# Log-gate sums carried as rows of the score operands, one-step normalisation helpers, and recurrent states kept at pairs of chunks

## The chip, the cores and the metric

The kernel runs on one core of a Trainium2 chip. The metric is the device time of one execution in microseconds (us). TensorE is PE in the profile (its weight loads PEld), VectorE is DVE, ScalarE is ACT, GpSimd is POOL, and SyncE, which issues the DMAs, is SP.

## The reference, cut to what matters

A sequence of 512 tokens of width 1024 goes through two blocks. The first has a short-convolution layer and a forgetting-attention layer (16 heads of 64), each followed by a gated feed-forward layer and a layer norm. The second normalises by root mean square, mixes with four latent-attention heads and four gated-linear-attention heads that run forward and backward, and ends in a feed-forward layer and an output gate. All of it is in float32. The parts that the change touches:

```
# forgetting attention, a head h: F is the running sum of log f over the tokens
logits[t, s] = q[t] . k[s] * 0.125 + F[t] - F[s]      (s <= t, else -inf)
p = softmax(logits)

# gated linear attention, chunks of 64 tokens, in each of two directions
b = cumsum(log f) inside a chunk
o_intra = (mask * (q*exp(b-b_mid)) @ (k*exp(b_mid-b)).T) @ v
state   = exp(b_last) * state + (k*exp(b_last-b)).T @ v       # one step for each chunk
o_inter = (q*exp(b)) @ state_before

rms_norm(x)   = x * rsqrt(mean(x*x) + eps) * g
layer_norm(x) = (x - mean) * rsqrt(var + eps) * g + b
```

## The kernel before

**Layout.** Activations lie transposed, features on the 128 partitions and the 512 tokens along the row. A product in full precision is three matmuls of operands split into a high and a low part (`mm3`); weights stream from DRAM in units of eight 128x128 blocks (`_make_unit`): one DMA into `raw`, a cast to `whi` on ACT, and a subtraction to `wlo` on DVE or POOL.

**Order.** Nothing is issued as it is written. A recorder takes down every operation, `cost` (line 291) gives it a price by engine and size, and `plan` (line 365) is a list scheduler that walks through a modelled time: each engine takes the ready operation that stands first in the program, buffers and PSUM banks are counted in ledgers, and a tensor-tensor operation of DVE can be given to POOL when DVE's queue is long (`to_pool`). The result is one fixed order for each engine, SP's DMAs included. All instructions therefore carry one line in the profile, 575, and are told apart by the names of their tiles. Changing an operation or a price redraws the order everywhere.

**Forgetting attention** (`fox_block`, line 1238). The projections that give the log gates (`pf`), two key tiles (`pk0`, `pk1`) and the first values (`pv`) run together over the tiles `hk` that the layer norm before delivers; `rest` then makes the query inputs `hq`. The gate goes through log-sigmoid to a running sum `F` of 16 heads (line 1267), which is stored to DRAM as `fd` and also transposed by PE into `fneg` (lines 1274 to 1278). The score step `fox_scores` (line 1390) handles a pair of heads: for each head the row of `F` is read back from `fd` to all 128 partitions (`Fb`), `Fm` adds the causal mask of a diagonal block, and for each of four query blocks `i` two matmuls write S (with the opposite sign), DVE builds the deviation `G` in one or two `tensor_scalar` operations and then adds it to S and takes the minimum in one `tensor_tensor_reduce`; ACT exponentiates:

```
if i:
    nc.vector.tensor_scalar(G[:, :i * P], Fb[hh][:, :i * P], self.fneg[:, i, h:h + 1], None, ALU.add)
nc.vector.tensor_scalar(G[:, tb], Fm[hh][:, tb], self.fneg[:, i, h:h + 1], None, ALU.add)
nc.vector.tensor_tensor_reduce(G[:, :N], s[:, :N], G[:, :N], 1.0, BIG, ALU.add, ALU.min, negm[hh][:, i:i + 1])
```

The second of the two score matmuls multiplies the low part of k (`k..l`, one tile for both heads) with a query tile (`q..az`, `q..bz`) whose other 64 rows are zero (`fox_k`, `fox_q`). `fox_values` transposes the probabilities (`tp`, `PT`) and multiplies with the values (`po`). The eight pairs are recorded so that the scores of pair f+1, the keys and queries of pair f+2 and the values of pair f interleave.

**Normalisation** (`newton_rsqrt`, line 793; `rms_rstd`, line 809). Four layer norms (each in two halves of 256 tokens) and 17 root-mean-square norms (512 tokens) take a logarithm, an exponential and a square on ACT and then three operations on DVE (tiles `..a`, `..r`); a root-mean-square norm first moves its PSUM sum to `..v` on DVE. `split_scaled` (line 881) makes the high part of a normalised tile on ACT, its full value `..e` on DVE, and the low part on DVE.

**Gated linear attention** (`gla_prep`, `gla_scores`, `gla_states`, lines 1818 to 1905). For each of 4 heads and 2 directions there are 8 chunks: 7 matmuls with 64 rows give the chunk products `..kv`, the states `..st` follow one another on DVE (one copy on ACT, then 6 multiply-adds), and each state enters the output `gpo` by a matmul with 64 columns. `B2_ORDER` (line 30) is the recorded order of the steps of these heads and of the four latent-attention heads (`proj`, `score`, `value`).

Of the kernel before, what the change touches and what calls it, by code (L numbers as in the profile page):

```python
# [6 lines left out]
F32 = mybir.dt.float32  # L7
# [152 lines left out]
class Part:  # L160


    def __init__(self, tile, key, rows):
        self.tile, self.key, self.rows, self.cast = tile, key, rows, None
# [5 lines left out]
    def region(self):  # L170
        return (*self.rows, 0, 1)
# [7 lines left out]
class DramRef(TileRef):  # L179
    def __getitem__(self, key):  # L180
        k = key[0] if isinstance(key, tuple) else key
        rows = (k, k + 1) if isinstance(k, int) else (k.start, k.stop)
        return Part(self, key, rows)

    def all(self):
        return Part(self, None, (0, self.shape[0]))
# [7 lines left out]
class Recorder:  # L194
# [96 lines left out]
    def cost(self, op, ins, outs):  # L291
# [11 lines left out]
        if op.eng == "PE":  # L303
# [3 lines left out]
            if dt == F32:  # L307
                return 4 + max(4 * size / 2.4, 156)
# [280 lines left out]
class Build:  # L589
# [203 lines left out]
    def newton_rsqrt(self, v, name, r=None):  # L793
# [3 lines left out]
        r0 = self.f(name + "r0", sh)  # L797
        self.act(r0, v, AF.Ln)
        self.act(r0, r0, AF.Exp, scale=-0.5)
        a = self.f(name + "a", sh)  # L800
        nc.scalar.activation(a, r0, AF.Square)
# [79 lines left out]
    def split_scaled(self, d, g, b, hl, sl, name):  # L881
# [4 lines left out]
        nc.vector.tensor_scalar(e, d[:, sl], g, b, ALU.mult, ALU.add)  # L886
# [37 lines left out]
    def setup(self):  # L924
# [37 lines left out]

        self.cmask = self.c("cmask", (P, 1, P))
        nc.gpsimd.memset(self.cmask, 0.0)
        nc.gpsimd.affine_select(self.cmask, self.cmask, [[0, 1], [-1, P]], ALU.is_ge, 1.0e30,
                                base=0, channel_multiplier=1)
        self.one_col = self.c("one_col", (P, 1))
        nc.gpsimd.memset(self.one_col, 1.0)
        self.tiny_col = self.c("tiny_col", (P, 1))
        nc.gpsimd.memset(self.tiny_col, 1.2e-19)  # L970
# [263 lines left out]
    def fox_block(self, kva, qa, rest, ln):  # L1234
# [33 lines left out]
        fd = self.dram("fd", (H, T))  # L1268
        nc.sync.dma_start(fd.all(), F)
# [4 lines left out]
        tp = self.ps("s", "Ftp", (P, 4, H))  # L1274
# [7 lines left out]
        probs = self.fox_scores(0, q[0], ks[0], fd)  # L1282
        q.append(self.fox_q(1, qa))
        for f in range(8):
# [8 lines left out]
            if f < 7:  # L1293
                probs = self.fox_scores(f + 1, q[f + 1], ks[f + 1], fd)
# [18 lines left out]
    def fox_k(self, f, kva, pk=None):  # L1313
# [3 lines left out]
        ka, kb, kl = (self.r(f"k{f}{n}") for n in ("a", "b", "l"))  # L1317
        top, bot = slice(0, 64), slice(64, P)
        if pk is None:
            pk = self.out(f"pk{f}")  # L1320
            self.gemm_all([("w_k", f, pk)], kva)
        for ps, sl in pk:
            nc.scalar.copy(kb[:, sl], ps)
            nc.scalar.copy(ka[top, sl], ps[top])
            nc.scalar.copy(ka[bot, sl], ps[top])
            nc.vector.tensor_tensor(kl[:, sl], ps, kb.bitcast(F32)[:, sl], ALU.subtract)
            nc.scalar.copy(kb[top, sl], ps[bot])
        return ka, kb, kl
# [43 lines left out]
    def fox_q(self, f, qa):  # L1372
# [6 lines left out]
        q = [self.r(f"q{f}{n}") for n in ("a", "b", "az", "bz")]  # L1379
        halves = slice(0, 64), slice(64, P)  # L1380
        for hh in range(2):
            own, other = halves[hh], halves[1 - hh]

            nc.gpsimd.memset(q[2 + hh].bitcast(F32)[other], 0.0)
# [667 lines left out]
```

## Time and profile before

| | before |
|---|---|
| median of 3 runs | 1939.76 us (1939.32 to 1940.83) |
| profiled execution, its own time | 1939.52 us |
| span of its profile | 1937.8 us |
| PE, PEld busy | 1893.9 us (98%), 1593.3 us (82%) |
| DVE, ACT, POOL busy | 1284.3 (66%), 817.4 (42%), 190.3 us (10%) |
| mean granted TensorE clock | 0.989 of full speed |
| forgetting attention | about 572 to 843 us of the span |
| mixer of the second block | about 1215 to 1486 us of the span |

The span runs from the first to the last instruction; the time of the execution is 1.7 us longer. A busy PE says that a matmul was in flight, not that it ran at full clock: the windows below carry the granted clock of each stretch beside the busy time. A matmul of float32 operands shows as two records.

### The profile page before, as it was taken

The page shows a single profiled execution, that of the slowest core. Times are in us where ns is not written, and L with a number is a line of the kernel's source. Part 1 is how long each engine was busy: PE and PEld are TensorE (multiplying, and loading weights), DVE is VectorE, ACT ScalarE, POOL GpSimd, SP SyncE. Part 2 cuts the span into 40 slices and gives each one's busy share as a digit, 9 for nine tenths or more (in the row PEclk, how much of TensorE's full clock was granted, in tenths as well). Part 3 has the DMA queues.
Part 4 walks back from the last instruction along what each step waited for, and adds up shares of the span by engine and source line. Part 5 has one row for each costly group of instructions (what it writes and reads, how often), then busy time and mean ns, then how long its engine had stood idle before and what let it go on. Part 6 is the DMA issues. An engine that isn't in the chain of part 4 may idle for free.

```text
span 1937.8 us, 24555 instructions
## 1 busy us (share of the span) xinstructions
PE 1893.9 (98%) x9382; PEld 1593.3 (82%) x9382; DVE 1284.3 (66%) x2208; ACT 817.4 (42%) x1344; POOL 190.3 (10%) x148
## 2 busy tenths in 40 slices
PE   9999999999999989999999999999999999999999
PEld 7888888888888778898888888877877888888887
DVE  8877976566579788894533335999898644334445
ACT  5322523122346667553322232686684533123333
POOL 0000100000010332210000000132151000000000
PEclk9999999999999899999999999999998999999999
DMA  9675277566434112323222222422111222222232
GB/s 350 224 249 173 99 241 251 187 233 228 142 108 153 58 64 88 120 66 131 99 94 96 97 98 79 140 82 82 44 55 44 98 98 98 98 98 94 94 139 76
DMA packets 76470, 245.55 MB, mean 127 GB/s; under 512 B 8496, under 2 KB 9776, under 8 KB 76352
## 3 DMA queue, kind: packets, MB, share of 16 engines
q1 hardware_dynamic: 76352, 243.98, 36.6%
q8 instruction: 73, 1.20, 0.3%
q14 instruction: 45, 0.37, 0.1%
HBM read 235.53 MB, written 8.42 MB: 126 GB/s over the span
## 4 chain that ended last, share of the span: by engine, by line
PE 57%; DVE 7%; ACT 2%; issue 1%; DVEq 0%; ACTq 0%
PE pu L575 12%; PE pg L575 12%; PE pd L575 9%; PE gt L575 4%; PE ffn_down L575 2%; PE wo L575 2%; PE pl L575 2%; PE attn_o L575 1%; DVE axr L575 1%; PE pv L575 1%; PE po L575 1%; PE pq L575 1%; PE MS L575 1%; PE tp L575 1%; PE pk L575 1%; PE S L575 1%
## 5 line engine op out<-in xcount | busy, mean ns | idle before, releaser
L575 ACT CAST whi<-raw 128x1024 fp32r<-128x1024 f32 (+1 forms) x313 | 326.1, 1043 | 598.5 <-PE pd L575 139.1
L575 DVE TENSOR_TENSOR wlo<-raw,whi 128x1024 fp32r<-128x1024 f32 (+1 forms) x286 | 349.8, 1224 | 321.0 <-ACT whi L575 316.9
L575 POOL TENSOR_TENSOR wlo<-raw,whi 128x1024 fp32r<-128x1024 f32 x27 | 65.4, 2423 | 1281.7 <-ACT whi L575 1251.5
L575 DVE CUSTOM_DVE_ANT_0 aj<-ada,cact,adab 128x1024 bf16<-128x1024 f32 x96 | 126.3, 1322 | 30.0 <-DMA ada<-in_wada 29.4
L575 DVE TENSOR_TENSOR s<-pu,s 128x512 f32<-128x512 f32 x44 | 30.1, 689 | 76.5 <-PE pu L575 76.5
L575 DVE TENSOR_TENSOR S<-S,sq 128x512 f32<-128x512 f32 (+1 forms) x62 | 36.7, 591 | 1.6 <-ACT sq L575 1.4
L575 ACT ACTIVATE s<-s 128x512 f32<-128x512 f32 x22 | 13.9, 632 | 54.1 <-DVE s L575 54.1
L575 ACT ACTIVATE s<-pg 128x512 f32<-128x512 f32 x44 | 26.0, 591 | 23.2 <-PE pg L575 23.0
L575 DVE CUSTOM_DVE_ANT_0 G<-S,G 128x128 f32<-128x128 f32 (+3 forms) x64 | 30.6, 484 | 1.6 <-PE S L575 0.9
L575 DVE TENSOR_TENSOR xr<-pd,xr 128x512 f32<-128x512 f32 x16 | 11.0, 690 | 26.9 <-PE pd L575 26.9
L575 DVE TENSOR_SCALAR G<-Fm,fneg 128x128 f32<-128x128 f32 x64 | 25.9, 410 | 0.9 <-PE po L575 0.5
L575 ACT ACTIVATE sq<-axr 128x256 f32<-128x256 f32 (+1 forms) x33 | 15.1, 466 | 23.1 <-DVE axr L575 23.1
L575 DVE TENSOR_SCALAR G<-Fb,fneg 128x128 f32<-128x128 f32 (+2 forms) x48 | 23.6, 491 | 1.3 <-ACT Pa L575 0.6
L575 DVE TENSOR_TENSOR s<-pg,rfr 128x512 f32<-128x512 f32 x22 | 15.2, 691 | 12.0 <-PE pg L575 12.0
L575 DVE TENSOR_TENSOR u<-pu,rfr 128x512 f32<-128x512 f32 x22 | 15.2, 691 | 11.8 <-PE pu L575 11.7
L575 POOL TENSOR_TENSOR Fm<-Fb,cmask 128x512 f32<-128x512 f32 x14 | 18.6, 1334 | 27.7 <-DVE PT_2l L575 9.1
L575 PE MATMUL tp<-ident,Pa 128*128 128x128 f32 x64 | 17.2, 294 | 3.2 <-DVE Pa L575 3.1
L575 PE MATMUL pg<-hm0l,whi 128*128 128x512 f32 (+1 forms) x48 | 18.0, 376 | 1.9 <-DVE hm0l L575 1.9
L575 PE MATMUL pg<-hm0h,whi 128*128 128x512 f32 (+1 forms) x48 | 18.0, 378 | 1.3 <-ACT hm0h L575 1.3
L575 ACT ACTIVATE Pa<-G,negm 128x128 f32<-128x128 f32 (+1 forms) x32 | 16.2, 505 | 6.8 <-DVE negm L575 4.7
L575 ACT ACTIVATE sq<-x 128x256 f32<-128x256 f32 (+1 forms) x19 | 9.8, 518 | 21.6 <-DVE x L575 21.5
L575 PE MATMUL pg<-hm0h,wlo 128*128 128x512 f32 (+1 forms) x48 | 18.0, 376 | 0.6 <-DVE wlo L575 0.6
(3680 smaller groups left out, 6298.7 us busy)
## 6 DMA issues: line engine op xcount, KB each, us to landing
raw<-in_wpack SPq DMA_DIRECT2D x309, 512.0 KB, 3.5
ada<-in_wada SPq DMA_DIRECT2D x96, 512.0 KB, 4.2
ada<-in_wada SPq DMA_DIRECT2D x32, 256.0 KB, 6.0
Fb<-fd SPq DMA_DIRECT2D x16, 256.0 KB, 4.5
x<-in_xT SPq DMA_DIRECT2D x8, 256.0 KB, 6.0
pd<-pple SPq DMA_DIRECT2D x8, 256.0 KB, 6.0
xd<-x SPq DMA_DIRECT2D x8, 256.0 KB, 2.6
axr<-xd SPq DMA_DIRECT2D x8, 256.0 KB, 5.1
```

The costliest lines, as they stand in the source:

```text
L575: getattr(getattr(nc, op.unit), op.name)(*[get(x) for x in op.args], **{k: get(x) for k, x in op.kw.items()})
```

## The change

- **Scores.** `F` is split into a high and a low part and both rows of a head are stored in `fd`. A new helper `beside` makes, for each head, the q and k tiles of the second score matmul: 64 rows hold the low part of k (or the query), and of the other 64 rows, 32 are all -1 (k) or +1 (q) and 32 are zero but for the two rows of `F`, which a DMA brings from `fd`. The matmul itself then adds F[s] - F[t]. `Fb`, `Fm`, `fneg`, the transposes of `F` and all the `tensor_scalar` operations on `G` go; the `tensor_tensor_reduce` reads a fixed mask of 512 columns, shifted by block. There are now two low-part tiles of k in place of one.
- **Norms.** `newton_rsqrt` takes two operations on DVE in place of three, ACT scales once more, and the root-mean-square norms read their sum from PSUM with no `..v`. The full value `..e` in `split_scaled` moves from DVE to ACT.
- **States.** Keys and queries are decayed to the edges of pairs of chunks, so that there are 3 matmuls with 128 rows for the products, 2 multiply-adds after one copy, and 3 matmuls with 128 columns into `gpo` for each head and direction. The part from one chunk of a pair to the other is computed in `gla_scores` by 4 more matmuls of 64x64, and two POOL memsets in `mla_scores` open these regions in the mask. `gla_prep` has six products of 256 elements where it had two of 512, and one small product for the pair's decay.
- **Prices** in `cost`: float32 matmuls of few columns 193 for 156, `tensor_tensor_reduce` 112 for 180, a price for the scan.

```diff
@@ cost
-                return 4 + max(4 * size / 2.4, 156)
+                return 4 + max(4 * size / 2.4, 193)
...
-            return 180 + 1.0417 * size + 61 * cols
+            return 112 + 1.0417 * size + 61 * cols
...
+        if n == "tensor_tensor_scan":
+            return 68 + 2.0833 * size
@@ newton_rsqrt(self, v, name, r=None, n=1.0, eps=0.0)
         nc.scalar.activation(a, y, AF.Square)
-        nc.vector.tensor_tensor(a, a, v, ALU.mult)
-        nc.vector.tensor_scalar(a, a, -0.5, 1.5, ALU.mult, ALU.add)
+        nc.scalar.mul(y, y, -0.5 / n)
+        if eps:
+            nc.vector.scalar_tensor_tensor(a, v, n * eps, a, ALU.add, ALU.mult)
+        else:
+            nc.vector.tensor_tensor(a, a, v, ALU.mult)
...
-        nc.vector.tensor_tensor(r, a, r0, ALU.mult)
+        nc.vector.scalar_tensor_tensor(r, a, 3.0 * n, y, ALU.subtract, ALU.mult)
@@ rms_rstd
-        v = self.f(name + "v")
-        nc.vector.tensor_scalar(v, s, 1.0 / n, EPS, ALU.mult, ALU.add)
-        return self.newton_rsqrt(v, name)
+        return self.newton_rsqrt(s, name, n=float(n), eps=EPS)
@@ split_scaled
-        nc.vector.tensor_scalar(e, d[:, sl], g, b, ALU.mult, ALU.add)
+        nc.scalar.activation(e, d[:, sl], AF.Identity, bias=b, scale=g)
@@ fox_block
-        fd = self.dram("fd", (H, T))
-        nc.sync.dma_start(fd.all(), F)
+        fd = self.dram("fd", (H, 2, T))
+        for i, x in enumerate(self.split(F, "Fx")):
+            nc.sync.dma_start(fd[0:H, i], x.bitcast(F32))
...
-        for i in range(4):
-            nc.tensor.transpose(tp[:, i, :], F[:, i * P:(i + 1) * P], self.ident[:H, :H])
-        self.fneg = self.c("fneg", (P, 4, H))
-        nc.scalar.mul(self.fneg, tp, -1.0)
@@ fox_k
+        low = [self.beside(2 * f + hh, "k", -1.0) for hh in range(2)]
         for ps, sl in pk:
...
+            for hi, lo, own, other in ((ka, low[0], top, bot), (kb, low[1], bot, top)):
+                nc.scalar.copy(hi[own, sl], ps[own])
+                nc.vector.tensor_tensor(lo[own, sl], ps[own], hi.bitcast(F32)[own, sl], ALU.subtract)
+                nc.scalar.copy(hi[other, sl], ps[own])
+    def beside(self, h, name, first):
+        nc = self.nc
+        t = self.r(f"{name}z{h}")
+        o = 64 * (1 - h % 2)
+        ones, sums = (o, o + 32) if name == "k" else (o + 32, o)
+        nc.gpsimd.memset(t.bitcast(F32)[ones:ones + 32], first)
+        nc.gpsimd.memset(t.bitcast(F32)[sums:sums + 32], 0.0)
+        nc.sync.dma_start(t.bitcast(F32)[sums:sums + 2], self.fd[h])
+        return t
@@ fox_scores
-            nc.sync.dma_start(t, fd[h:h + 1, :].to_broadcast((P, T)))
...
-            nc.vector.tensor_tensor(m.chunks(P), t.chunks(P), self.cmask.to_broadcast((P, 4, P)), ALU.add)
...
-                nc.tensor.matmul(s[:, :W], q[2 + hh][:, tb], k[2][:, :W], start=False, stop=True)
+                nc.tensor.matmul(s[:, :W], q[2 + hh][:, tb], k[2 + hh][:, :W], start=False, stop=True)
...
-                if i:
-                    nc.vector.tensor_scalar(G[:, :i * P], Fb[hh][:, :i * P], self.fneg[:, i, h:h + 1],
-                                            None, ALU.add)
-                nc.vector.tensor_scalar(G[:, tb], Fm[hh][:, tb], self.fneg[:, i, h:h + 1], None, ALU.add)
-                nc.vector.tensor_tensor_reduce(G[:, :N], s[:, :N], G[:, :N], 1.0, BIG, ALU.add, ALU.min,
+                nc.vector.tensor_tensor_reduce(G[:, :N], s[:, :N], self.cmask[:, T - N:], 1.0, BIG, ALU.add, ALU.min,
@@ gla_prep
-            nc.vector.tensor_tensor(bl, bl, k, ALU.mult)
...
+            nc.vector.tensor_tensor(kx, lp[:, :, near], k3[:, :, near], ALU.mult)
+            nc.vector.tensor_tensor(lp[:, :, far], lp[:, :, far], k3[:, :, far], ALU.mult)
+            nc.vector.tensor_tensor(lp[:, :, near], kx, bp[:, :, e1:e1 + 1].to_broadcast((P, 4, 64)), ALU.mult)
+            nc.vector.tensor_tensor(qx, bp[:, :, far], q3[:, :, far], ALU.mult)
...
-            nc.vector.tensor_tensor(qb, b, q, ALU.mult)
+            nc.vector.tensor_tensor(qp[:, :, near], bp[:, :, near], q3[:, :, near], ALU.mult)
+            nc.vector.tensor_tensor(qp[:, :, far], qx, bp[:, :, e0:e0 + 1].to_broadcast((P, 4, 64)), ALU.mult)
+            nc.vector.tensor_tensor(dec, bp[:, :, e0], bp[:, :, e1], ALU.mult)
@@ gla_scores
+            for p in range(4):
+                sl = slice(p * 64, (p + 1) * 64)
+                nc.tensor.matmul(pa[near, p, far], x[:, 0, sl], x[:, 1, sl], start=True, stop=True)
@@ gla_states
-            for c in order[:7]:
-                rw = slice(64 * (c % 2), 64 * (c % 2) + 64)
-                nc.tensor.matmul(pk[c % 2][:, c // 2, :], kd[rw, c // 2, :], v[rw, c // 2, :],
-                                 start=True, stop=True)
+            for c in order[:3]:
+                nc.tensor.matmul(pk[:, c, :], kds[d][:, c, :], v[:, c, :], start=True, stop=True)
...
-                    nc.vector.scalar_tensor_tensor(new, S, b[:, col:col + 1], kvc, ALU.mult, ALU.add)
+                    nc.vector.scalar_tensor_tensor(new, S, dec[:, c:c + 1], pk[:, c, :], ALU.mult, ALU.add)
...
-                nc.tensor.matmul(po[:, n * 64:(n + 1) * 64], S, qb[:, n * 64:(n + 1) * 64],
-                                 start=False, stop=(d == 1 and i == 6))
+                nc.tensor.matmul(po[:, n * P:(n + 1) * P], S, qb[:, n * P:(n + 1) * P],
+                                 start=False, stop=(d == 1 and i == 2))
```

## Rows read from the trace of the kernel before

**Rows 1.** The page's first part: busy time, share of the span, instructions of each engine.

```profile
PE 1893.9 (98%) x9382; PEld 1593.3 (82%) x9382; DVE 1284.3 (66%) x2208; ACT 817.4 (42%) x1344; POOL 190.3 (10%) x148
```

**Rows 2.** Busy time by stretch (length, then PE, PEld, DVE, ACT, POOL), granted clock, DMA.

```profile
600.00:616.00 16.00, 13.54 (x61) 11.04 (x60) 15.84 (x31) 10.60 (x22) 0.00 (x0) 0.89 0.34 124
...
636.00:660.00 24.00, 20.79 (x105) 16.20 (x104) 18.01 (x58) 10.56 (x29) 2.67 (x3) 0.79 0.06 22
...
680.00:700.00 20.00, 14.67 (x65) 11.24 (x64) 15.58 (x42) 8.87 (x18) 7.00 (x8) 0.83 0.08 28
...
1424.00:1480.00 56.00, 48.59 (x292) 40.74 (x289) 51.66 (x98) 33.45 (x68) 21.88 (x17) 0.85 0.13 44
```

**Rows 3.** The same view, 40 us around each of four layer norms: one, and the sum.

```profile
560.00:600.00 40.00, 37.04 (x296) 35.48 (x295) 37.80 (x92) 26.61 (x50) 4.96 (x4) 1.00 0.20 70
...
sum 160.00, PE 148.78 PEld 138.25 DVE 149.21 ACT 92.56 POOL 14.91; mean PE 37.19 PEld 34.56 DVE 37.30 ACT 23.14 POOL 3.73
```

**Rows 4.** What PE waited for, 600 to 700 us: total, times, longest.

```profile
PE tp L575 <- DVE Pm L575: 2.9, 1, 2.9
PE Ftp L575 <- DVE F L575: 2.5, 1, 2.5
```

**Rows 5.** The same view, whole span: waits in the mixer's end.

```profile
PE MS L575 <- DVE kns3l L575: 2.4, 1, 2.4
...
PE gpo L575 <- DVE gl20st L575: 1.9, 1, 1.9
PE MS L575 <- DVE mx L575: 1.8, 1, 1.8
```

**Rows 6.** The page's costliest groups: what builds the deviations, busy time and mean ns.

```profile
L575 DVE TENSOR_SCALAR G<-Fm,fneg 128x128 f32<-128x128 f32 x64 | 25.9, 410 | 0.9 <-PE po L575 0.5
...
L575 DVE TENSOR_SCALAR G<-Fb,fneg 128x128 f32<-128x128 f32 (+2 forms) x48 | 23.6, 491 | 1.3 <-ACT Pa L575 0.6
```

**Rows 7.** Instructions of DVE in order of time (start, length), 678 to 684 us.

```profile
678.24 2.57 DVE L575 TENSOR_SCALAR G<-Fb,fneg 128x384 f32<-128x384 f32 x1
...
683.19 0.41 DVE L575 TENSOR_SCALAR G<-Fb,fneg 128x384 f32<-128x384 f32 x1
```

**Rows 8.** The same view, POOL.

```profile
678.20 2.40 POOL L575 TENSOR_TENSOR wlo<-raw,whi 128x1024 fp32r<-128x1024 f32 x1
```

**Rows 9.** The view by tile: one low part of k, one memset of a query tile.

```profile
L575 DVE TENSOR_TENSOR k4l<-pk,k4b x1: 692/692/692, 688.0 to 688.0; 128x512 fp32r<-128x512 f32 x1
...
L575 POOL MEMSET q4az<- x1: 522/522/522, 109.8 to 109.8; 64x512 f32 x1
```

**Rows 10.** DMA issues: count, KB each, median us to landing.

```profile
Fb<-fd SPq DMA_DIRECT2D x16, 256.0 KB, 4.5
...
fd<-F SPq DMA_DIRECT2D x1, 32.0 KB, 1.6
```

**Rows 11.** Groups by shape in the mixer, PE: records, busy us, mean ns.

```profile
L575 PE MATMUL gpo<-gl01qb,gl01st 128*128 128x64 f32 x14 | 1.7, 275 | 0.0
...
L575 PE MATMUL gl00kv<-gv,gs00kd 64*128 64x128 f32 x14 | 1.2, 286 | 0.0
...
L575 PE MATMUL gs00A<-gl00qi,gl00bm 128*128 128x128 f32 x8 | 1.1, 275 | 0.0
```

**Rows 12.** Groups by shape in the mixer, DVE: one state's multiply-adds.

```profile
L575 DVE SCALAR_TENSOR_TENSOR gl20st<-gl20st,sg_0e,gl20kv 128x128 f32<-128x128 f32 x6 | 2.0, 332 | 0.0
```

**Rows 13.** Instructions of DVE in order of time, 1442 to 1449 us.

```profile
1442.46 0.69 DVE L575 TENSOR_SCALAR rqn3v<-rqn3ps 128x512 f32<-128x512 f32 x1 [0.90 <-PE rqn3ps L575]
...
1443.67 0.69 DVE L575 TENSOR_TENSOR gl30qb<-sg_0e,sq3e 128x512 f32<-128x512 f32 x1
...
1448.35 0.41 DVE L575 TENSOR_SCALAR rqn3a<-rqn3a 128x512 f32<-128x512 f32 x1
```

**Rows 14.** The same view, DVE, 572 to 575 us.

```profile
572.89 0.40 DVE L575 TENSOR_SCALAR hk00e<-x,kvG,kvB 128x256 f32<-128x256 f32 x1
```

**Rows 15.** The same view, ACT, 572 to 574 us.

```profile
571.93 0.60 ACT L575 ACTIVATE hk0h<-x,kvB,kvG 128x256 fp32r<-128x256 f32 x1 [0.29 <-DVE x L575]
```

More of the change, by code (lines that the diff above doesn't have):

```diff
@@ L160, with __init__ @@
 class Part:
-    def __init__(self, tile, key, rows):
-        self.tile, self.key, self.rows, self.cast = tile, key, rows, None
+    def __init__(self, tile, key, rows, cols):
+        self.tile, self.key, self.rows, self.cols, self.cast = tile, key, rows, cols, None
     def to_broadcast(self, shape):
@@ L170, in region @@
     def region(self):
-        return (*self.rows, 0, 1)
+        return (*self.rows, *self.cols)
     def real(self):
@@ L182, in __getitem__ @@
         rows = (k, k + 1) if isinstance(k, int) else (k.start, k.stop)
-        return Part(self, key, rows)
-    def all(self):
-        return Part(self, None, (0, self.shape[0]))
+        part = isinstance(key, tuple) and isinstance(key[1], int)
+        return Part(self, key, rows, (key[1], key[1] + 1) if part else (0, 1 << 30))
 class Op:
@@ L961, in setup @@
         nc.gpsimd.memset(self.onesd, 1.0 / D)
[L963 to L970, printed above, removed]
+        cols = self.c("cols", (P, 3))
+        self.one_col, self.eps_col, self.tiny_col = (cols[:, i:i + 1] for i in range(3))
+        for col, x in ((self.one_col, 1.0), (self.eps_col, EPS), (self.tiny_col, 1.2e-19)):
+            nc.gpsimd.memset(col, x)
     def warm_up(self):
@@ L1315, in fox_k @@
         nc.group = f"kv{f}"
-        ka, kb, kl = (self.r(f"k{f}{n}") for n in ("a", "b", "l"))
+        ka, kb = (self.r(f"k{f}{n}") for n in "ab")
         top, bot = slice(0, 64), slice(64, P)
@@ L1377, in fox_q @@
         pq = pq[0][0]
-        q = [self.r(f"q{f}{n}") for n in ("a", "b", "az", "bz")]
+        q = [self.r(f"q{f}{n}") for n in "ab"] + [self.beside(2 * f + hh, "q", 1.0) for hh in range(2)]
         halves = slice(0, 64), slice(64, P)
@@ L1853, in gla_scores @@
         for d in range(2):
-            qi, ki, kd_, _, _ = prep[d]
+            qi, ki, kd_, _, _, x = prep[d]
             nm = f"gs{h}{d}"
+            near, far = slice(64 * d, 64 * d + 64), slice(64 - 64 * d, P - 64 * d)
             pa = self.ps("s", nm + "A", (P, 4, P))
@@ L1873, in gla_states @@
         po = self.ps("o", f"gpo{h}")
-        first = True
+        for p in range(4):
+            nc.tensor.matmul(po[:, p * P:(p + 1) * P], v[:, p, :], kds[2][:, p, :],
+                             start=(p == 0), stop=False)
         for d in range(2):
-            b, qb = prep[d][3:]
+            dec, qb = prep[d][3:5]
             nm = f"gl{h}{d}"
-            kd = kds[d]
-            last = 63 * (1 - d)
-            order = list(range(8)) if d == 0 else list(range(7, -1, -1))
-            pk = [self.ps("s", nm + f"kv{i}", (P, 4, P)) for i in range(2)]
-            for c in order[:7]:
-                rw = slice(64 * (c % 2), 64 * (c % 2) + 64)
-                nc.tensor.matmul(pk[c % 2][:, c // 2, :], kd[rw, c // 2, :], v[rw, c // 2, :],
-                                 start=True, stop=True)
-            for p in range(4 if d == 0 else 0):
-                nc.tensor.matmul(po[:, p * P:(p + 1) * P], v[:, p, :], kds[2][:, p, :],
-                                 start=first, stop=False)
-                first = False
-            st = [self.f(nm + f"st{i}", (P, 4, P)) for i in range(2)]
+            order = list(range(4)) if d == 0 else list(range(3, -1, -1))
+            pk = self.ps("s", nm + "kv", (P, 4, P))
+            for c in order[:3]:
+                nc.tensor.matmul(pk[:, c, :], kds[d][:, c, :], v[:, c, :], start=True, stop=True)
+            st = self.f(nm + "st", (P, 4, P))
@@ L1892, in gla_states @@
             S = None
-            for i, c in enumerate(order[:7]):
-                new = st[i // 4][:, i % 4, :]
-                kvc = pk[c % 2][:, c // 2, :]
+            for i, c in enumerate(order[:3]):
+                new = st[:, i, :]
                 if S is None:
-                    nc.scalar.copy(new, kvc)
+                    nc.scalar.copy(new, pk[:, c, :])
                 else:
-                    col = c * 64 + last
-                    nc.vector.scalar_tensor_tensor(new, S, b[:, col:col + 1], kvc, ALU.mult, ALU.add)
+                    nc.vector.scalar_tensor_tensor(new, S, dec[:, c:c + 1], pk[:, c, :], ALU.mult, ALU.add)
```

53 lines of the change are left out of this document (30 added, 23 removed).

## The prediction

> **What bounds the kernel now.** I read the page's busy times first: PE is in flight for 98% of the span [rows 1], so time can only come from PE's own work, from the 44 us in which it stands, or from stretches in which it runs at a lower clock. The busy time by stretch says where those are. In the feed-forward stages PE is full at full clock and nothing there is to be had. PE stands in two places. In the forgetting attention, three stretches between 600 and 700 us miss 2.46, 3.21 and 5.33 us of PE, 11.0 together, and their granted clock is 0.89, 0.79 and 0.83 [rows 2]. The clock has two levels, 2.4 and 1.2 GHz, so a mean of c over L us loses at most (1-c)L of work: 1.8, 5.0 and 3.4, together 10.2. In the end of the second block's mixer, 1424 to 1480 us, 7.4 us of standing and at most 0.15 x 56 = 8.4 us of clock are lost [rows 2]. The reader should see that in the first and the last of these DVE is nearly full. Third, four layer norms cost 160 - 148.8 = 11.2 us of standing [rows 3].
>
> The list of waits then says what PE stood for. In the attention it is DVE: probabilities not yet scaled (Pm, 2.9 us) and the running sum of the gates, whose transposes stand in PE's fixed order (2.5) [rows 4]. No wait for a DMA is in that list. In the mixer's end it is DVE again: a key's low part, a state, a maximum [rows 5]. So PE is the bound where it is full, and DVE's queue is the bound where it is not.
>
> **The change part by part.** *Scores.* The 112 `tensor_scalar` operations on G cost 25.9 + 23.6 = 49.5 us of DVE [rows 6], 6.2 us for each of eight pairs, ahead of the scaling on which PE waits. Added are one more subtraction to a low part of k for each pair and one for the split of F: nine at 0.69 us [rows 9], 6.2 us. Net 43 us of DVE over some 190 us of attention. PE's four transposes of F go, and with them the 2.5 us wait and what clock it cost. The number and shape of the score matmuls stay.
>
> Where that lands: with 6 us less of DVE for each pair, the scaling should be done before PE has used up the projections that the planner puts between; the three stretches hold 11.0 + 10.2 = 21.2 us. I take 16, three quarters, since the last waits of such a chain (transpose, cast, subtract, product of the values) stay as they are and the first pair still starts behind F. What is late next is that chain. Bounds 8 (only the longest wait of each kind and its clock) and 21.
>
> Some of the 49.5 us is collision. The same operation takes 0.41 us alone and 2.57 us when it starts just after a POOL subtraction of 2.40 us [rows 7, 8]. The Trainium skill (SBUF — State Buffer, "Who interferes with whom") says that a `tensor_scalar` in a two-port mode and a POOL instruction shut each other out for a whole instruction, also one that only writes, while an operation with two SBUF inputs minds only POOL instructions that read. The trace agrees on the first half; by the second the new memsets could hit only the scaling that is left, which is the third rival below.
>
> POOL's memsets grow from 2 to 8 for each pair, 64 in all. I cost them at nothing: they wait for no data, and the planner put the one shown at 109.8 us, in a stage with idle POOL, for a tile used some 600 us later [rows 9]. If that cover goes they cost up to 0.52 us each.
>
> DMAs: 16 broadcasts of 256 KB go, 32 loads of two rows and one more store come. SP has 17 more issues. Their landing lies between the small store's 1.6 us and the broadcast's 4.5 us [rows 10]; I take 4.5, as they share the queue with the weights. At the start, F, split (two operations, some 1.4 us), store 1.6 and load 4.5 put the first score matmul about 7.5 us after F. Today it doesn't wait for F at all, but its reduction does. The cover is the projections of the second pair's queries and the third pair's keys and queries. Costed at nothing; if the cover is gone, 7.5 us once, and what every later pair would pay is the last rival.
>
> *States.* For each head and direction PE now spends 1.2 us on products and 1.7 on the output [rows 11]. Afterwards: six matmuls at 1.1/4 = 0.275 us make 1.65, and four of 64x64, not in this trace, at 0.17 (a product row, 1.2/7) to 0.24 (a 64-column row, 1.7/7) make 0.69 to 0.97. Eight times a saving of 0.28 to 0.56 is 2.2 to 4.5 us. PE is full around them, so this counts in the time; I take 3.
>
> On DVE, 4 of 6 multiply-adds at 0.33 [rows 12] go, eight times: 10.6 us. Six products of 256 elements come for two of 512 at 0.69 [rows 13]; at 0.40, as the 256-element operation of rows 14, 8 x (2.4 - 1.4) = 8 us more (bounds 0.35, half of 0.69, and 0.69 itself). The mask's two small memsets and the waits between them and the mask's reads hide behind the score matmuls.
>
> *Norms.* Each of 17 root-mean-square norms loses 0.69 + 0.41 us on DVE [rows 13] and gains one ACT operation (0.60 by rows 15, which has fewer elements but two column operands). Fifteen lie in or just before the mixer: 16.5 us. So DVE loses 10.6 + 16.5 - 8 = 19 us in a stage where it is the fuller partner. In the stretch to 1480 us, with two heads' states and about four norms, that is some 7 of 51.7 us, and a state's chain has two steps for six. Of the 15.8 us lost there I take 6. Bounds: 14, and -3, because keys and queries of a pair pass one more product before the transposes.
>
> For a layer norm, 16 operations `..e` at 0.40 us [rows 14] leave DVE (37.3 of 40 us busy on average) and 16 x 0.60 = 9.6 us come to ACT (23.1 of 40) [rows 3, 15]. ACT has the room. But the low part then waits for two ACT operations in a row, 0.6 us later for the first tile, against one DVE operation less in the chain to the standard deviation. I take 2.5 us for the four, bounds -2 and 5.
>
> *Sum:* 16 + 3 + 6 + 2.5 = 27.5 us, against the profiled execution's own 1939.5 us (span 1937.8 and 1.7 around it; it stands 0.2 below the median of the runs): **1912.0 us**. The bounds alone give 1895 to 1934.
>
> **The rivals.**
> 1. *Only the attention gains.* The mixer's end is a chain through single operations, and the planner, given less DVE work, packs it no better: 16 + 3 = 19, 1920.5 us. For it: PE's waits there are on a state, a key and a maximum in turn [rows 5]. Against it: two of the three lie behind operations that go. 0.20.
> 2. *All of it comes.* 21 + 4.5 + 10 + 4 = 39.5, 1900 us. For it: the clock rises by itself when PE no longer stands. 0.12.
> 3. *The memsets take DVE's gain back.* 64 x 0.52 = 33 of the net 43 us, if each is placed in the attention and meets a scaling: the 16 us shrink to 4, 1924 us. Against it: rows 9. This is the page's rule at work, at its worst. 0.08.
> 4. *It evens out.* The new prices redraw every order; if the attention keeps its stretches behind another chain and the mixer its tail, some 4 us are left: 1936 us. 0.07.
> 5. *Slower.* The score matmul now waits for rows from DRAM, which stand in SP's one queue among weight loads that wait for a free buffer. If the rows of each pair land 4.5 us late, eight pairs lose 36 us: 1939.5 - 27.5 + 36 = 1948 us. It decides from 27.5/8 = 3.4 us late for each pair. For it: SP is in order and PE too. Against it: today's larger loads stand in the same queue and none is in the list of waits [rows 4, 10]; the rows of all later pairs are ready to be fetched as soon as the tile is there. 0.08. That the change fails to do what it says is not in question for the scores; for the norms, it would be rival 1.
>
> **How the numbers follow.** The forecast has 0.45. About 0.2% (3.9 us) is what a measurement of this kernel can tell from no change. Faster by more: 0.45 + 0.20 + 0.12 + 0.08 = 0.85; within it 0.07; slower 0.08. The range reaches from just below rival 2 to past rival 3 and the attention's lower bound (16 less 8, with 3 + 2.5 + 0 elsewhere: 1926), so 1899 to 1930; it leaves out rivals 4 and 5, 0.15.
>
> **What would show it.** Right: no group G<-Fb or G<-Fm, DVE some 40 us lower in 600 to 840 us; the waits for Pm and F gone and the clock near 1.0 from 600 to 700 us; the states' records down from 28 to 12 for each head and direction, with 8 new ones in the scores; a wait for a state gone from the mixer's end. Wrong: a score matmul waiting for a DMA; scalings of 1 us and more beside memsets; the stretch 1424 to 1480 us with its clock still at 0.85; PE waiting longer for the low part of the first normalised tile.

## The result: 33.9 us faster, and the profile after

| | before | after |
|---|---|---|
| median | 1940.3 us (1939.32 to 1941.76) | 1906.39 us (1906.07 to 1906.92) |
| ratio, 95% interval | | 0.9825, 0.9808 to 0.9842 |
| profiled execution: own time, span | 1939.52, 1937.8 us | 1906.07, 1904.3 us |
| mean granted clock | 0.989 | 0.995 |

The row of before has one run more than the table ahead of the prediction. The forecast was 1912.0 us, the range 1899 to 1930. The page's first part of the changed kernel, to be read against [rows 1]:

```profile
PE 1870.2 (98%) x9314; PEld 1575.8 (83%) x9314; DVE 1224.7 (64%) x2019; ACT 855.8 (45%) x1425; POOL 171.7 (9%) x185
```

To see where the time went I cut the span at the same events in every kernel. The *attention* runs here from the last matmul of the first feed-forward stage (`ffn_down0`) to the last of `attn_o`, the *mixer* from the first matmul on `hx0h` to the last of the output product `wo`. Busy time by stretch, attention then mixer (columns as in [rows 2]), before:

```profile
570.96:843.63 272.67, 257.70 (x1536) 224.49 (x1536) 238.01 (x604) 172.21 (x393) 67.35 (x43) 0.96 0.28 96
1215.49:1529.21 313.72, 303.49 (x1585) 252.55 (x1586) 281.69 (x491) 209.63 (x375) 75.17 (x53) 0.97 0.21 74
```

The same two stretches of the changed kernel:

```profile
568.92:818.09 249.17, 246.36 (x1532) 219.08 (x1532) 199.53 (x481) 183.29 (x419) 26.03 (x24) 1.00 0.26 88
1189.81:1495.83 306.02, 292.78 (x1521) 241.83 (x1522) 274.23 (x464) 219.34 (x391) 75.51 (x60) 0.97 0.22 76
```

Of the 33.5 us by which the span is shorter, the attention gave 23.5 and the mixer 7.7. Another 2.6 lie ahead of the first feed-forward stage, which now starts at 201.15 us for 203.76; the remaining stretches give 0.4 back. In the attention PE's standing (length less busy) fell from 15.0 to 2.8 us and the clock from 0.96 to 1.00. The three stretches of [rows 2], same times on the clock, now:

```profile
600.00:616.00 16.00, 14.77 (x66) 11.82 (x66) 13.09 (x23) 15.73 (x32) 2.40 (x1) 1.00 0.39 132
636.00:660.00 24.00, 23.27 (x136) 19.61 (x135) 21.82 (x73) 20.50 (x61) 5.34 (x6) 1.00 0.19 67
680.00:700.00 20.00, 20.00 (x155) 19.25 (x154) 12.39 (x30) 10.52 (x28) 0.00 (x0) 1.00 0.18 62
```

PE's waits in the attention; those for Pm and F of [rows 4] are gone, and none is for a DMA:

```profile
PE S L575 <- DVE q0a L575: 1.1, 1, 1.1
PE S L575 <- DVE PT_1l L575: 0.7, 1, 0.7
PE pf L575 <- DVE hk0l L575: 0.4, 1, 0.4
```

DVE did not simply become idle. Its weight subtractions in the attention, by shape, before and after:

```profile
L575 DVE TENSOR_TENSOR wlo<-raw,whi 128x1024 fp32r<-128x1024 f32 x18 | 22.8, 1270 | 1.3 <-ACT whi L575 1.3
```

```profile
L575 DVE TENSOR_TENSOR wlo<-raw,whi 128x1024 fp32r<-128x1024 f32 x28 | 36.6, 1311 | 12.5 <-ACT whi L575 12.4
```

Ten of them moved to it from POOL, whose busy time in the attention fell from 67.4 to 26.0 us; POOL also lost the 14 mask additions `Fm` that it had there (18.6 us), which the prediction did not count. DVE lost 38.5 us net. Beside less of POOL's work the long scalings went too: none of the 64 takes over 0.49 us, where one took 2.52 beside a subtraction on POOL.

The mixer's end is the opposite. PE's waits from 1380 us on, beside which [rows 5] is to be laid:

```profile
PE gpo L575 <- ACT gl20st L575: 6.3, 1, 6.3
PE MS L575 <- ACT kns3h L575: 2.1, 1, 2.1
PE gpo L575 <- DVE mx L575: 1.1, 1, 1.1
```

The stretch that answers to 1424 to 1480 us of [rows 2]:

```profile
1400.00:1450.00 50.00, 38.37 (x233) 30.50 (x232) 48.24 (x83) 34.47 (x68) 26.41 (x22) 0.83 0.15 56
```

11.6 us of standing and 0.17 x 50 = 8.5 of clock, where it was 7.4 and 8.4. In this account of busy and standing time, about 11 us less of PE's work is all that the mixer gained, and 3 of it were lost again. The stretch is one of the signs of being wrong that the prediction named: its clock is still low, 0.83.

### The profile page after: what moved, and what is told of

Its sections match the earlier page's. It is cut to its first block, busy times and chain, and to the rows that moved or that the text cites. A ratio compares the mean times of both kernels' runs of the same rounds, so it can differ in the third digit from the quotient of the medians.

```text
span 1904.3 us, 24367 instructions
## 1 busy us (share of the span) xinstructions
PE 1870.2 (98%) x9314; PEld 1575.8 (83%) x9314; DVE 1224.7 (64%) x2019; ACT 855.8 (45%) x1425; POOL 171.7 (9%) x185
## 4 chain that ended last, share of the span: by engine, by line
PE 89%; DVE 6%; ACT 3%; issue 1%; DMA 0%; SPq 0%; DVEq 0%; ACTq 0%
PE pg L575 19%; PE pu L575 19%; PE pd L575 13%; PE ffn_down L575 5%; PE gt L575 4%; PE pv L575 2%; PE wo L575 2%; PE gb L575 2%; PE gc L575 2%; PE vv L575 2%; PE pk L575 2%; PE pq L575 2%; PE pl L575 2%; PE conv_out L575 1%; PE attn_o L575 1%; PE S L575 1%
## 5 line engine op out<-in xcount | busy, mean ns | idle before, releaser
L575 DVE TENSOR_TENSOR wlo<-raw,whi 128x1024 fp32r<-128x1024 f32 (+1 forms) x294 | 362.2, 1233 | 345.2 <-ACT whi L575 341.5
L575 POOL TENSOR_TENSOR wlo<-raw,whi 128x1024 fp32r<-128x1024 f32 x19 | 46.0, 2420 | 1158.6 <-ACT whi L575 1158.6
L575 DVE CUSTOM_DVE_ANT_0 G<-S,cmask 128x128 f32<-128x128 f32 (+3 forms) x64 | 28.1, 487 | 2.5 <-PE S L575 1.9
L575 DVE TENSOR_TENSOR s<-pg,rfr 128x512 f32<-128x512 f32 x22 | 15.2, 691 | 11.9 <-PE pg L575 11.9
L575 DVE TENSOR_TENSOR u<-pu,rfr 128x512 f32<-128x512 f32 x22 | 15.2, 691 | 11.5 <-PE pu L575 11.4
L575 POOL MEMSET kz<- 32x512 f32 x32 | 17.3, 539 | 33.9 <-PE pd L575 15.2
L575 PE MATMUL S<-kz,qz 128*128 128x256 f32 (+2 forms) x64 | 20.0, 331 | 0.0
L575 POOL MEMSET qz<- 32x512 f32 x32 | 16.6, 518 | 33.5 <-DVE ada L575 32.2
L575 PE MATMUL pg<-hm4l,whi 128*128 128x512 f32 (+1 forms) x48 | 17.9, 373 | 1.0 <-DVE hm4l L575 1.0
L575 PE MATMUL pg<-hm2l,whi 128*128 128x512 f32 (+1 forms) x48 | 17.9, 373 | 1.0 <-DVE hm2l L575 1.0
L575 DVE TENSOR_TENSOR gz<-gt,rxr 128x512 f32<-128x512 f32 x20 | 13.7, 683 | 7.8 <-PE gt L575 7.7
L575 PE MATMUL pg<-hm1l,whi 128*128 128x512 f32 (+1 forms) x48 | 17.9, 374 | 0.4 <-DVE hm1l L575 0.4
```

Of the source, the lines that this page charges most:

```text
L575: getattr(getattr(nc, op.unit), op.name)(*[get(x) for x in op.args], **{k: get(x) for k, x in op.kw.items()})
```

## The experiments

All times are medians, each against runs of before on the same chip (1939.5 to 1940.8 us). The two stage lengths come from the trace of each kernel's profiled execution. Where the text sets one of these kernels against the changed kernel, medians from different chips are compared.

| kernel | us | ratio to before, 95% | attention | mixer |
|---|---|---|---|---|
| before | 1940.3 | | 272.7 | 313.7 |
| after | 1906.39 | 0.9808 to 0.9842 | 249.2 | 306.0 |
| e_scores | 1925.12 | 0.9907 to 0.9937 | 256.4 | 315.4 |
| e_states | 1939.99 | 0.9994 to 1.0013 | 272.7 | 313.2 |
| e_norms | 1948.83 | 1.0025 to 1.0050 | 271.2 | 324.7 |
| e_prices | 1943.68 | 1.0007 to 1.0031 | 273.4 | 324.4 |
| x_noprices | 1912.60 | 0.9837 to 0.9870 | 254.4 | 305.2 |
| x_nonorms | 1917.55 | 0.9866 to 0.9896 | 264.3 | 302.1 |
| x_nostates | 1930.27 | 0.9931 to 0.9961 | 249.3 | 330.0 |
| x_edve | 1921.88 | 0.9890 to 0.9923 | 261.4 | 308.8 |
| b_rmsold | 1908.89 | 0.9823 to 0.9853 | 249.2 | 309.2 |
| f_dvefix | 1928.44 | 0.9924 to 0.9954 | 271.8 | 306.5 |
| b_state2 | 1910.98 | 0.9833 to 0.9862 | 249.2 | 310.2 |
| b_order | 1889.37 | 0.9717 to 0.9749 | 249.2 | 288.9 |

### One part alone on the kernel before

Scores (with `beside`, the two rows of `fd`, and all that goes with them):

```diff
-                if i:
-                    nc.vector.tensor_scalar(G[:, :i * P], Fb[hh][:, :i * P], ...
-                nc.vector.tensor_scalar(G[:, tb], Fm[hh][:, tb], ...
-                nc.vector.tensor_tensor_reduce(G[:, :N], s[:, :N], G[:, :N], ...
+                nc.vector.tensor_tensor_reduce(G[:, :N], s[:, :N], self.cmask[:, T - N:], ...
```

> The scores part alone, on the kernel before (prices, norms and states as before). Theory A, each part earns its gain in its own stage: about 1917 us, 23 us below before, since between the two traces the attention (first matmul on hk0h to the end of attn_o) shrank from 271.1 to 249.0 us; the half-speed stretches between 600 and 700 us gone; the waits for Pm and F gone. Theory B, most of the gain is the order that the planner redraws from the new prices: at most 12 us below before, 1928 us or more, and half-speed stretches remain in the attention.

15.0 us below before, 16.3 of them in the attention: between the two theories.

States (`gla_prep`, `gla_scores`, `gla_states` and the mask's memsets):

```diff
-            for c in order[:7]:
...
+            for c in order[:3]:
+                nc.tensor.matmul(pk[:, c, :], kds[d][:, c, :], v[:, c, :], start=True, stop=True)
```

> The states part alone, on the kernel before. Theory A: PE's own time in the mixer falls by some 10 us (9.1 on gpo and 4.9 on the chunk products less, 3.4 on the score tiles more, as between the two traces); what PE then waits at the mixer's end takes up to 3 back: 1929 to 1933 us. My prediction's term of 3 us would give 1937. Theory B: within 4 us of before.

Nothing. PE's busy time in the mixer did fall, from 303.5 to 294.6 us, but its standing rose from 10.2 to 18.5: the work went and the waits took its place.

Norms (`newton_rsqrt`, `rms_rstd`, `split_scaled`):

```diff
-        nc.vector.tensor_tensor(r, a, r0, ALU.mult)
+        nc.vector.scalar_tensor_tensor(r, a, 3.0 * n, y, ALU.subtract, ALU.mult)
...
-        nc.vector.tensor_scalar(e, d[:, sl], g, b, ALU.mult, ALU.add)
+        nc.scalar.activation(e, d[:, sl], AF.Identity, bias=b, scale=g)
```

> The norms part alone, on the kernel before: newton_rsqrt and rms_rstd in their new form, and the full value of the normalised tiles from ACT. Theory A: little, 1 to 3 us below before (1937 to 1939 us), 1.4 of it in the layer norm ahead of the attention, nothing in the mixer's end, whose half-speed time stayed at 17.07 us. My prediction's split gave it some 6: 2.5 in the layer norms and most of 6 in the mixer's end, 1934 us.

8.7 us slower, 11.0 of it in the mixer, although DVE has 6 us less work there. Neither theory.

Prices:

```diff
-                return 4 + max(4 * size / 2.4, 156)
+                return 4 + max(4 * size / 2.4, 193)
...
-            return 180 + 1.0417 * size + 61 * cols
+            return 112 + 1.0417 * size + 61 * cols
...
+        if n == "tensor_tensor_scan":
+            return 68 + 2.0833 * size
```

> The three prices of the planner alone, on the kernel before; no operation changes. Theory A: within 3 us of before, either sign, and the first 200 us as before. Theory B: 5 us or more below before; in particular the 2.6 us that the changed kernel gains before its first feed-forward stage appear here.

3.5 us slower by the medians. The profiled execution was 1948.56 us, 4.9 above the median; single runs of this kernel spread from 1939.8 to 1950.2. One part of theory B holds: the first feed-forward stage starts 2.0 us earlier. The mixer is 10.7 us longer in that execution, with no operation changed.

The four gains are 15.0, 0.1, -8.7 and -3.5 us: 2.9 together, for a whole of 33.9. The parts don't add, so the next runs took one part away from the whole.

### One part taken away from the changed kernel

The edits are those above, undone one at a time.

> The changed kernel without the new prices (scores, norms and states). The four parts alone gave 15.0 (scores), 0.1 (states), -8.7 (norms) and -3.6 us (prices): together 3, not the 33.9 of the whole. Theory P, the missing gain needs the new prices, without which the planner still places the shorter operations by the old figures: 1922 us or more. Theory N, the scores need the norms part (their first pair starts behind the running sum F, which the layer norm's DVE work delays) and the mixer's end is a matter of how each redrawn order falls: the attention stays at 249 to 252 us, the time within 1900 to 1920 us by the mixer's end alone.

6.2 us slower than the changed kernel, 5.3 of it in the attention and 2.0 ahead of the first feed-forward stage. Theory P, at 1922 or more, falls. Of theory N the time holds, the attention not: 254.4 us for 249 to 252.

> The changed kernel without the norms part (prices, scores and states). Theory N: the scan of F lies as late after the layer norm as with the scores alone (614 us there against 605.8 in the changed kernel), the attention takes 254 to 257 us in place of 249.2, measured from the end of the first feed-forward stage to the end of attn_o. Theory P: 249 to 251 us as in the changed kernel. The mixer: DVE has some 16 us more in it; if the norms' term of 6 us was right, the mixer is 5 us or more longer than in the changed kernel.

The attention is 15.2 us longer, more than theory N said. The sum does start late, as it said: 612.7 us, 43.1 after the end of the feed-forward stage where the changed kernel has 36.9. But the prices have a part in the 15.2. With the old prices the same norms part is worth 2.0 us in the attention (256.4 in e_scores, 254.4 in x_noprices); the states part, in which these two differ besides, leaves the attention as it is (272.7 us in e_states and in before, 249.3 in x_nostates where the changed kernel has 249.2). So the norms help the attention much only in the order that the new prices draw. The mixer is 4.0 us *shorter* than the changed kernel's: there the norms part cost time, against my term, by which the mixer should have been 5 us or more longer.

> The changed kernel without the states part (prices, scores and norms). PE has its 10.6 us of work in the mixer back. If the mixer is limited by PE's work, it takes 10 us longer than the changed kernel's, 1916 us; if its end is limited by chains through DVE and ACT, as the states alone (0.1 us of gain) say, it takes about the same, 1906 to 1909 us. The attention is the changed kernel's, 249 us, in both.

The mixer is 24 us longer, not 10. Its row:

```profile
1190.67:1520.69 330.02, 311.31 (x1585) 258.23 (x1586) 282.46 (x468) 218.80 (x391) 67.08 (x44) 0.95 0.22 71
```

18.7 us of standing, and a clock of 0.95 over 330 us. The same states part was worth 0.1 us alone. So in the mixer a part has no fixed worth of its own: lengths of 302 to 330 us come from PE work that differs by 11 us at most.

### DVE's work, with the order held

The parts above redraw the planner's order each time. Here every engine keeps the order of the changed kernel, and the `tensor_scalar` operations are issued again (from the mask; the reduction then overwrites what they wrote):

```diff
     for i, op in enumerate(order):
+        if op.name == "tensor_tensor_reduce" and op.args[0].tile.name.startswith("G"):
+            G, _, m = op.args[:3]
+            n = G.shape[1]
+            for a, b in ((0, n - P), (n - P, n)):
+                if b > a:
+                    nc.vector.tensor_scalar(get(G[:, a:b]), get(m[:, a:b]), 1.0, None, ALU.add)
```

> The changed kernel with every engine's order as it is, but ahead of each reduction of a score tile DVE again makes one or two tensor_scalar operations of the old shapes on its G tile (from the mask; the reduction does not use them): 112 operations, by the changed kernel's rows for the same shapes (0.29, 0.35, 0.42 us) about 35 us of DVE. Nothing of F comes back: no transposes, no broadcasts. Theory D, DVE's time ahead of the scaling is what PE waited for: the attention grows by 12 us or more (249.2 to 261 or more) and half-speed stretches return. Rival, the running sum, its transposes and the collisions with POOL were the cost: under 5 us.

The attention took 271.8 us: of the 23.5 that the change gave there, 22.7 went again. Its row:

```profile
569.47:841.31 271.84, 257.14 (x1533) 222.52 (x1532) 232.95 (x593) 187.26 (x419) 26.07 (x24) 0.98 0.25 81
```

PE stands for 14.7 us, where it stood for 2.8, and the clock is down to 0.98. What was added, by shape:

```profile
L580 DVE TENSOR_SCALAR G<-cmask 128x128 f32<-128x128 f32 x80 | 23.5, 311 | 0.2
...
L580 DVE TENSOR_SCALAR G<-cmask 128x256 f32<-128x256 f32 x16 | 6.6, 412 | 0.0
L580 DVE TENSOR_SCALAR G<-cmask 128x384 f32<-128x384 f32 x16 | 6.1, 381 | 0.0
```

And what PE waits for in the attention then (`S` behind `negm` is a score matmul behind an earlier reduction):

```profile
PE S L581 <- DVE negm L581: 3.9, 6, 1.2
PE tp L581 <- DVE Pa L581: 3.1, 2, 2.6
...
PE tp L581 <- DVE Pm L581: 2.0, 1, 2.0
```

Nothing of F came back, so its transposes and broadcasts are not needed for the loss. DVE's time ahead of the reductions and the scaling is enough for it: theory D. The order was drawn without these operations, though; what they would cost in an order drawn with them is shown by no run. Part of that time is still collision with POOL, whose 26 us are unchanged: the longest of the 112 operations took 2.47 us, the median 0.22.

### Which of the norms the attention needs

```diff
-        nc.scalar.activation(e, d[:, sl], AF.Identity, bias=b, scale=g)
+        nc.vector.tensor_scalar(e, d[:, sl], g, b, ALU.mult, ALU.add)
```

> The changed kernel with only the full value ..e of the normalised tiles back on DVE. Without the whole norms part the attention took 264.3 us in place of 249.2. Theory E, it is this one operation: the 16 of a layer norm stand on DVE ahead of the scan of F, on whose rows the score matmuls now wait: attention 259 us or more, the first reduction of a score tile after 622 us (618.2 in the changed kernel). Rival, it is the shorter chain to the standard deviation: attention 249 to 252 us.

One kind of operation makes 12.2 of the 15.2 us. In the attention it is 24 operations, not the 16 of the expectation: the eight tiles `hq` of 512 columns have a full value too (0.53 us each on DVE). The running sum in the changed kernel, then in this one (duration, start):

```profile
L575 DVE TENSOR_TENSOR_SCAN F<-one_t,zfe x1: 1211/1211/1211, 605.8 to 605.8; 16x512 f32<-16x512 f32 x1
```

```profile
L575 DVE TENSOR_TENSOR_SCAN F<-one_t,zfe x1: 1202/1202/1202, 610.2 to 610.2; 16x512 f32<-16x512 f32 x1
```

Measured from the end of the feed-forward stage (568.9 and 568.3 us) the sum starts 5 us later, and the first reduction of a score tile 6 us later, at 623.5 for 618.2. That this delay makes the 12 us is not shown, and e_scores speaks against it as the whole cause: there the sum starts 42.6 us after the stage and the first reduction 54.0, here 41.9 and 55.2, and yet the attention takes 256.4 us there and 261.4 here. Each of these orders was drawn anew.

### The root-mean-square norms alone in the old form

```diff
-        return self.newton_rsqrt(s, name, n=float(n), eps=EPS)
+        v = self.f(name + "v")
+        nc.vector.tensor_scalar(v, s, 1.0 / n, EPS, ALU.mult, ALU.add)
...
+        nc.vector.tensor_scalar(a, a, -0.5, 1.5, ALU.mult, ALU.add)
+        nc.vector.tensor_tensor(r, a, y, ALU.mult)
```

> The changed kernel with the old form of the root-mean-square norms alone (sum moved to ..v, three operations on DVE); layer norms and the full value from ACT stay new. My prediction's term: DVE relieved of these 16.5 us is worth up to 6 us in the mixer, so without it the mixer takes 310 us or more in place of 306.0, 1910 us or more in all. Theory K, ACT's queue, full from 1412 to 1424 us in the changed kernel, is what the new form lengthens (four operations of a norm in a row there): the mixer takes 302 to 304 us as it did without the norms part (302.05), 1902 to 1904 us. The attention takes 249 us in both.

309.2 us, between the two. Theory K falls. DVE has 13.6 us more in the mixer, and the mixer is 3.2 us longer. In x_edve it is 2.8 us longer with none of its operations changed, so the 3.2 can't be told from a new order.

### The longest wait, and the order

The 6.33 us wait, in the changed kernel's instructions in order of time (start, length), PE:

```profile
1415.13 0.38 PE L575 MATMUL gl20kv<-gv,gs20kd 128*128 128x128 f32 x2
...
1424.28 0.79 PE L575 MATMUL gpo<-gl20qb,gl20st 128*128 128x128 f32 x2 [6.33 <-ACT gl20st L575]
1427.14 0.80 PE L575 MATMUL MS<-kns3h,qns3h 128*128 128x512 f32 x1 [2.07 <-ACT kns3h L575]
```

The state's copy on ACT:

```profile
1423.03 1.03 ACT L575 CAST whi<-raw 128x1024 fp32r<-128x1024 f32 x1
1423.96 0.26 ACT L575 COPY gl20st<-gl20kv 128x128 f32<-128x128 f32 x1
```

Its product was done at 1415.5 us, 8.4 earlier; the copy stood in ACT's queue. That looks like the thing to mend:

```diff
-... score3 value2 prep3 state2 gout1 intra3 state3
+... score3 value2 state2 prep3 gout1 intra3 state3
```

> The changed kernel with one step moved in the recorded order: state2 before prep3. In the changed kernel PE stands 6.33 us for a copy of a first state (gl20st) whose product was done at 1415.7 us but which ACT reaches at 1423.96, behind the exponentials of prep3 and a weight cast; and 17.1 us run at half speed around it. Theory Q, the copy's place in ACT's order is what costs: the wait goes, and with it up to 6.3 us and what clock it cost (up to 8.5): 1894 to 1901 us. Theory R, the tail of the mixer is full of chains, and the next (the last head's preparation, now later) takes its place: 1903 us or more.

4.6 us slower, theory R. The wait left the head of the list, and 4.7 us for a tile of the next head's preparation (`gl31x`) and 4.7 for a weight cast ahead of `wo` came. The last row of PE above suggests why the copy was no lever: the matmul after the state's waits until 1427.14 for a key's high part, which does not hang on the copy.

So not one wait but the whole arrangement was left to test. The projections of the linear heads (`gt`) are the largest work of PE in the mixer that waits for no chain. Their busy time up to the first matmul into an output `gpo`, and from there to the last state's, changed kernel:

```profile
1189.81:1380.53 190.72, 113.69 (x480) 1.00 0.22 78
1380.53:1449.25 68.72, 0.00 (x0) 0.88 0.20 70
```

All of it is used up before these outputs begin, and nothing of it is left beside the states' chains. The last kernel records the same steps in another order:

```diff
-B2_ORDER = """gate1 proj0 gate0 score0 prep0 proj1 score1 gate2 intra0 value0 value1 proj2 gate3 state0 gout0
-prep1 score2 intra1 state1 prep2 intra2 proj3 score3 value2 prep3 state2 gout1 intra3 state3
-gout3 value3 gout2"""
+B2_ORDER = """gate1 proj0 gate0 score0 prep0 intra0 proj1 score1 gate2 state0 value0 value1 gate3 proj2 gout0
+prep2 score2 prep1 intra1 state1 value2 intra2 state2 proj3 prep3
+score3 intra3 gout1 value3 state3 gout2 gout3"""
```

> The changed kernel with another recorded order of the second block's steps: intra0 and state0 before gate2's followers, prep2 before prep1, value2 and state2 before proj3, value3 before state3, both last heads' outputs at the end. No operation changes, so PE's work in the mixer stays at about 284 us (284.2 in the changed kernel); the other 21.8 of its 306.0 are standing (13.2) and half speed (8.5). Theory O, these 21.8 belong to the order in which ready work falls, not to one chain that every order has: the mixer takes 300 us or less and the time is 1900 us or less. Rival, the chain of the last latent-attention head (norm, scores, maximum, value, output product) sets the end whatever the order: the mixer at 303 us or more, 1903 us or more.

1889.37 us, 17.0 below the changed kernel and 51.4 below before: it beats both. The mixer, and `gt` cut in the same way:

```profile
1190.44:1479.36 288.92, 286.70 (x1521) 239.62 (x1522) 267.19 (x459) 219.60 (x391) 85.32 (x67) 1.00 0.24 81
```

```profile
1190.44:1335.21 144.77, 86.60 (x360) 1.00 0.28 95
1335.21:1442.08 106.87, 28.74 (x121) 1.00 0.17 60
```

PE stands for 2.2 us, and the clock is 1.00. A quarter of `gt` now lies beside the states. Theory O holds: nearly all of the 21.8 us of standing and half speed was the order's. Which of the moves did it was not taken apart.

## Why the prediction came out right, and where it was wrong

**Bound.** Right: PE full outside two places, DVE the bound in the attention. The order-held run shows it most directly: 33.4 us of DVE put back (232.95 for 199.53) cost 22.7, in an order drawn without them.

**Scores, 16 us.** Mechanism right, size low: 22 to 23, a little over the upper bound of 21. The failed words are "the last waits of such a chain ... stay as they are and the first pair still starts behind F": the stretches are all but empty. But the scores alone gave 16.3, and the rest came with the other parts. I costed `..e` on ACT only at the layer norms' edges (2.5 us for four), without the eight of `hq`, and not in DVE's queue behind it, where F's scan stands. That coupling is in no term. It is worth 12.2 us by x_edve, but with the old prices the whole norms part is worth 2.0, so it hangs on the order that the prices draw as much as on the operations. That the scores alone gave the forecast's 16 is agreement in the number: my term stood for the whole change.

**Memsets at nothing, rows' loads at nothing.** Right. The 32 row loads were issued between 611.9 and 623.4 us, for all pairs, and PE waits for none; rival 5 had no place to act. Of the 64 new memsets the latest started at 622.9 us. The page's groups show one half:

```profile
L575 POOL MEMSET kz<- 32x512 f32 x32 | 17.3, 539 | 33.9 <-PE pd L575 15.2
```

None met a scaling, so rival 3 fell on its "against". What memsets do to one stands in the trace of before, where those of the second block's tiles `cmk` and `at` fell beside the scalings of the attention; DVE, then POOL, in order of time:

```profile
688.97 1.39 DVE L575 TENSOR_SCALAR Pm<-Pm,rs 128x256 f32<-128x256 f32 x1
...
691.20 0.34 DVE L575 TENSOR_SCALAR Pm<-Pm,rs 128x256 f32<-128x256 f32 x1
```

```profile
688.72 0.53 POOL L575 MEMSET cmk<- 128x512 f32 x1
689.18 0.53 POOL L575 MEMSET at<- 128x512 f32 x1
689.65 0.12 POOL L575 MEMSET cmk<- 128x8 f32 x1
689.69 0.53 POOL L575 MEMSET at<- 128x512 f32 x1
```

A scaling of 0.34 us took 1.39 and ended at 690.36 us, the last memset at 690.22. So rival 3's mechanism is real here, and only the place of the new memsets kept it out.

**States, 3 us of PE.** Mis-sized: about 11. The new side of the sum, 8 x (1.65 + 0.69) = 18.7 us, was measured at 18.8 (output 8.1, products 7.0, the score tiles' growth 3.7), but its two halves miss: outputs and products took 15.1 for 13.2, and the score tiles grew by 3.7 for 5.5, since two of the old ones had run partly at half speed (434 and 410 ns for 275). The four 64x64 matmuls themselves took the forecast 0.7 us, once 0.9. The old side, 8 x (1.2 + 1.7) = 23.2, took [rows 11], two of the cheapest of eight heads and directions, for all. Others of the same group before, by shape:

```profile
L575 PE MATMUL gpo<-gl20qb,gl20st 128*128 128x64 f32 x14 | 3.5, 390 | 2.0 <-DVE gl20st L575 1.9
L575 PE MATMUL gpo<-gl21qb,gl21st 128*128 128x64 f32 x14 | 3.2, 421 | 0.0
L575 PE MATMUL gpo<-gl00qb,gl00st 128*128 128x64 f32 x14 | 2.6, 266 | 0.1
```

The eight sum to 19.0 for the output and 10.9 for the products, 29.9 in all. The first two ran largely at half speed (390 and 421 ns for 275); the third at full speed, but its matmuls lay spread from 1410.6 to 1415.1 us and overlapped less.

**Mixer's end, 6 us.** Wrong, and in sign: standing rose from 10.2 to 13.2 us in the mixer and the half speed stayed. The sign that I named for it, a wait for a state gone, failed: one of 1.9 us became one of 6.3. The failed step is "in a stage where it is the fuller partner", read as if relief of DVE there would reach PE. The root-mean-square norms' part was worth 3.2 us by b_rmsold, no more than a new order alone can make (2.8 in x_edve), and the order around the chains moves the stage by 17. The term that it cancelled against was the states': 3 + 6 forecast, 7.7 measured. That sum is right by luck.

**Layer norms, 2.5 us.** About 1.1: PE's gaps from the last matmul of a stage to the first of the next shrank from 1.3, 1.6, 2.1 and 1.1 to 1.3, 0.2, 2.4 and 1.1 us.

**Not costed:** the prices. Ahead of the first feed-forward stage the four kernels without them gain 0.3 to 0.7 us, all with them 1.8 to 2.7.

**Rivals.** 1 and 2 each had half: the attention of rival 2, the tail of rival 1 ("packs it no better").

## What to carry to other kernels

Where a planner draws the order, a part's gain alone says little: four parts gave 2.9 us one by one and 33.9 together. Test a cause with the order held, as with DVE's work here, and price a group from all its instances, not one. Where PE stands behind chains, look for where independent work was spent before them (one run here, its moves not separated); the longest wait in the list may only hide the next.

## What was not expected of the hardware

In the mixer's end some operations of DVE took over twice their time. Two of them and one that did not, changed kernel, DVE, in order of time:

```profile
1418.92 1.65 DVE L575 TENSOR_TENSOR qt<-qro,rqn3r 64x512 f32<-64x512 f32 x1
...
1422.64 1.72 DVE L575 SCALAR_TENSOR_TENSOR rkn3r<-rkn3a,rkn3r 128x512 f32<-128x512 f32 x1
...
1426.36 0.68 DVE L575 TENSOR_TENSOR kt<-kro,rkn3r 128x512 f32<-128x512 f32 x1
```

POOL beside them:

```profile
1418.52 1.50 POOL L575 TENSOR_TENSOR gl30bm<-gl30bm,gz 128x512 f32<-128x512 f32 x1 [1.45 <-ACT gl30bm L575]
1422.54 1.27 POOL L575 TENSOR_TENSOR gl31qi<-gl31qi,sq3e 128x512 f32<-128x512 f32 x1 [2.52 <-ACT gl31qi L575]
```

The third, with no POOL beside it, takes 0.68, and so does the first one's operation in the other three heads (0.68 to 0.69 us). My prediction had looked for such collisions only at `tensor_scalar`. The Trainium skill (SBUF — State Buffer, "Who interferes with whom") says that a DVE instruction with two SBUF inputs contends with a POOL instruction that reads SBUF; the trace agrees.

Single runs of one kernel can differ with the granted clock: ten runs of e_prices span 10.4 us, with mean clocks from 0.985 to 0.993, four of b_order 0.7 us, its profiled run at 0.999.
